# Sparse attention with all operands padded to the full 128x128 array, and one compressed-branch product for both groups

## The chip, the cores and the metric

One NeuronCore of a Trainium2 chip runs the whole layer in one launch. The metric is the device time of the program in microseconds; lower is better. The engines are TensorE (PE; its weight loads are listed as PEld), VectorE (DVE), ScalarE (ACT), GpSimd (POOL) and SyncE (SP), which here only starts transfers.

## The reference

A decoder layer over 256 tokens of width 2048, batch 1: a layer norm, then one projection into three head groups, their outputs joined and projected back, a layer norm, a convolutional feed-forward part (width 5632), a layer norm. The three groups are a gated linear recurrence (1024 channels), sparse attention (8 query heads of width 64 that share 2 key/value groups g), and cross-attention into 256 memory tokens (4 heads of width 128).

The sparse attention has, for each head, three branches: over compressed blocks of keys and values, over selected blocks, and over a window. With 256 tokens there are 4 blocks to select and 16 may be chosen, and the window is 512 wide, so the last two are both causal attention over all keys, each with its own keys and values:

```python
s_c = jnp.einsum('bghqd,bgnd->bghqn', qc, k_cmp) * scale      # 15 compressed blocks
p_c = masked_softmax(s_c, cmp_end[None, :] <= t[:, None])
o_c = jnp.einsum('bghqn,bgnd->bghqd', p_c, v_cmp)
o = gc[..., 0:1] * o_c + gc[..., 1:2] * o_s + gc[..., 2:3] * o_w
```

## The kernel before

All large weights stream through PE in chunks of 128x1024 fp32 (`chunk`, `run`). SyncE loads a chunk into `raw`; ScalarE rounds it to `wH` (L127), VectorE takes the rest `wL = raw - wH` (L135), two chunks ahead of use. The activations are split in the same way, and each product is made of three: high by high (L194), high weight by low activation (L195), low weight by high activation (L197). A chunk of the projection is 8 tiles of 128x128, each with 256 moving columns: 24 products. The L205, L206 and L208 products do the same with the activations as stationary operand.

Attention work is written as Python generators that are put into the list `bg`. After each chunk `pump` takes one step of each live generator, oldest first, and admits one new one, so the steps of several heads stand in one round, behind one chunk. The order of every engine's instructions follows from this by construction; engines wait for one another only by semaphores.

A head of the sparse attention (`nsa_head`, for 128 queries q, group g and head j within the group) has five steps: the score products (L675, and L676, which adds the causal mask by an identity matrix), softmax (L680 to L684), scaling by sum and gate (L686 to L689), transposes (L695) and their copy to `PT`, value products (L704) into the output bank `outs[q]`. Score products use 64 rows of the array, since a head is 64 wide: group 0 lies in partitions 0 to 63, group 1 in 64 to 127. Value products use 64 columns, since they write the 64 partitions of their group. A plain fp32 product is issued as two passes, a transpose as one. The second 128 queries have twice the keys and so four value products instead of two. There are 16 heads in all (8 for each half of the queries). The first of a half opens the output bank by a product with zeros (L701).

The compressed branch (`nsa_cmp`, for q and g) works in the same five steps: mask (L641) and four score products over 15 blocks (L643), softmax, scaling into `pc`, one transpose (L659), ScalarE copies of its four diagonal blocks into `pcd`, one value product for the four heads of the group (L664). The step of group 1 then splits the finished bank `outs[q]` into `oH` and `oL`. The PSUM tiles concerned are `sc` (two banks), `tp` (two) and `o` (one). The order of the generators is: eight heads of the first half as their queries arrive (`done_q`), two compressed, eight heads of the second half, two compressed, four memory heads.

Keys, values, compressed keys and compressed values are put in place by `done_kk`, `done_vg` and `cmp_rest`. The buffer `lruI` holds memory tokens at first, and later an operand of the recurrence. The kernel's last lines write zeros into a few buffers ahead of all work and convert masks on GpSimd.

Of the kernel before, what the change touches and what calls it, by code (L numbers as in the profile page):

```python
# [21 lines left out]
F32 = mybir.dt.float32  # L22
F32R = mybir.dt.float32r
BF = mybir.dt.bfloat16
AF = mybir.ActivationFunctionType
OP = mybir.AluOpType
AX = mybir.AxisListType
# [3 lines left out]
S = 256  # L31
# [24 lines left out]
def hymba_layer(ctx, tc, x, memT, params, rows, wab, w1, wmem, win, wvg, wout, wup, wdn, out):  # L56
    nc = tc.nc
    V, A, G, T = nc.vector, nc.scalar, nc.gpsimd, nc.tensor

    fix = ctx.enter_context(tc.tile_pool(name="fix", bufs=1))  # L60
# [17 lines left out]
    negh = fix.tile([128, 1], F32, name="negh")  # L78
    identb = fix.tile([128, 128], BF, name="identb")
    diagb = fix.tile([128, 2, 128], BF, name="diagb")  # L80
    cmaskb = fix.tile([128, 2, 60], BF, name="cmaskb")
    ident = prm[:, _P["ident"]]

    def P(name, i=0, n=1):
        s = _P[name].start + i
        return prm[:, s:s + n] if s < NP1 else prm2[:, s - NP1:s - NP1 + n]
# [99 lines left out]
    def split_act(dh, dl, src):  # L186
        A.activation(dh, src, AF.Copy)  # L187
        V.tensor_sub(dl, src, dh.bitcast(F32))  # L188
# [209 lines left out]
    def done_q(a, bank):  # L398
        if a == 0:
            qns[0] = mx.tile([128, 4, S], F32, name="qn")  # L400
        A.activation(qns[0][:, a, :], bank, AF.Copy)
        for g in range(2):
            bg.append(nsa_head(0, g, a))
        if a == 3:
            for g in range(2):
                bg.append(nsa_cmp(0, g))
            for g in range(2):
                for j in range(4):
                    bg.append(nsa_head(1, g, j))
            for g in range(2):  # L410
                bg.append(nsa_cmp(1, g))

    blkt = {}

# [12 lines left out]
                        src[g * 64:g * 64 + 64, hb:hb + 15, :, par],  # L427
                        P(pe, hb * 8, 8)[q][:, None, :].to_broadcast([64, 15, 8]), op=OP.add)

    kk = mx.tile([128, 2, S], F32, name="kk")  # L430

    def done_kk(a, bank):
        A.activation(kk[:, a, :], bank, AF.Copy)

    vv = mx.tile([128, 2, 256], F32, name="vv")
    gates = mx.tile([128, 2, 24], F32, name="gates")
    vacc = {}

    def done_vg():
        for m in range(2):  # L440
            A.activation(vv[:, m, :], vacc[m][:, :256], AF.Copy)
        for m in range(2):
            A.activation(gates[:, m, :], vacc[m][:, 256:NVG], AF.Exp, scale=-1.0)
        V.tensor_scalar(gates, gates, 1.0, None, op0=OP.add)
        V.reciprocal(gates, gates)
# [14 lines left out]


    kcmp = mx.tile([128, 32], F32, name="kcmp")
    vcmp = mx.tile([128, 2, 64], F32, name="vcmp")
    hidv = mx.tile([64, 2, 4, 32], F32, name="hidv")
    hidk = mx.tile([64, 32], F32, name="hidk")

    def cmp_mm(a):
# [8 lines left out]
    def cmp_rest(a, ps):  # L476
        if a == 0:
            A.activation(hidk[:, :30], ps[:64, :30], AF.Gelu_apprx_tanh)
        else:
            for g in range(2):  # L480
                A.activation(hidv[:, g, :, 0:15],
                             ps[:64, g * 15:(g + 1) * 15][:, None, :].to_broadcast([64, 4, 15]), AF.Gelu_apprx_tanh)
        yield
        ps2 = pp.tile([128, 512], F32, name="tp", bufs=2)
        if a == 0:
            T.matmul(ps2[:, :30], P("w2k", 0, 128)[:64], hidk[:, :30], start=True, stop=True)
            V.tensor_copy(kcmp[:, :30], ps2[:, :30])
        else:
            for g in range(2):
                T.matmul(ps2[:, g * 64:(g + 1) * 64], hidv[:, g].rearrange("p j n -> p (j n)"),  # L490
                         P("w2v", 0, 64)[:64], start=True, stop=True, skip_group_check=True)
            V.tensor_copy(vcmp, ps2[:, :128].rearrange("p (g d) -> p g d", g=2))
        yield


# [136 lines left out]
    def nsa_gates(q, g):  # L632
        return gates[:, q, g * 12:(g + 1) * 12].rearrange("p (j c) -> p j c", c=3)

    def nsa_cmp(q, g):
        qn = qns[0]
        rows_ = slice(g * 64, g * 64 + 64)
        qs = slice(q * 128, (q + 1) * 128)
        s = pp.tile([128, 512], F32, name="sc", bufs=2)
        sv = s[:, :60].rearrange("p (j n) -> p j n", j=4)  # L640
        T.matmul(s[:, :60], identb, cmaskb[:, q, :], start=True, stop=False, skip_group_check=True)  # L641
        for j in range(4):
            T.matmul(sv[:, j, :], qn[rows_, j, qs], kcmp[rows_, g * 15:(g + 1) * 15], start=False, stop=True,  # L643
                     skip_group_check=True)
        yield
        w = sm.tile([128, 12], F32, name="cw")
        cs = sm.tile([128, 4, 15], F32, name="cs", bufs=2)
        V.reduce_max(w[:, 0:4], sv, axis=AX.X)
        V.tensor_tensor(cs, sv, w[:, 0:4][:, :, None].to_broadcast([128, 4, 15]), op=OP.subtract)
        A.activation(cs, cs, AF.Exp, scale=NSA_SCALE)  # L650
        yield
        V.reduce_sum(w[:, 4:8], cs, axis=AX.X)
        V.reciprocal(w[:, 4:8], w[:, 4:8])
        V.scalar_tensor_tensor(w[:, 8:12], w[:, 4:8], P("cvalid", q), nsa_gates(q, g)[:, :, 0], op0=OP.mult, op1=OP.mult)
        V.tensor_tensor(pc.rearrange("p (j n) -> p j n", j=4)[:, :, :15], cs,
                        w[:, 8:12][:, :, None].to_broadcast([128, 4, 15]), op=OP.mult)
        yield
        tp = pp.tile([128, 4, 128], F32, name="tp", bufs=2)
        T.transpose(tp[:, 0, :], pc, ident)  # L659
        for j in range(4):  # L660
            r = slice(j * 32, j * 32 + 32)
            A.activation(pcd[r, j, :], tp[r, 0, :], AF.Copy)
        yield
        T.matmul(outs[q][rows_], vcmp[:, g, :], pcd, start=False, stop=True, skip_group_check=True)  # L664
        if g == 1:
            split_act(oH[:, 8:12, q * 128:(q + 1) * 128], oL[:, 8:12, q * 128:(q + 1) * 128], outs[q])
        yield

    def nsa_head(q, g, j):
        qn = qns[0]  # L670
        rows_ = slice(g * 64, g * 64 + 64)
        qs = slice(q * 128, (q + 1) * 128)
        nk = (q + 1) * 128
        s = pp.tile([128, 2, S], F32, name="sc", bufs=2)
        T.matmul(s[:, :, :nk], qn[rows_, j, qs], kk[rows_, :, :nk], start=True, stop=False, skip_group_check=True)  # L675
        T.matmul(s[:, :, nk - 128:nk], identb, diagb, start=False, stop=True, skip_group_check=True)  # L676
        yield
        w = sm.tile([128, 10], F32, name="sw", bufs=6)
        e = mx.tile([128, 2, S], F32, name="P", bufs=5)
        V.reduce_max(w[:, 0:2], s[:, :, :nk], axis=AX.X)  # L680
        V.tensor_scalar(w[:, 2:4], w[:, 0:2], -NSA_SCALE, None, op0=OP.mult)
        for b in range(2):
            A.activation(e[:, b, :nk], s[:, b, :nk], AF.Exp, bias=w[:, 2 + b:3 + b], scale=NSA_SCALE,
                         accum_out=w[:, 4 + b:5 + b])  # L684
        yield
        V.reciprocal(w[:, 6:8], w[:, 4:6])  # L686
        V.tensor_mul(w[:, 8:10], w[:, 6:8], nsa_gates(q, g)[:, j, 1:3])
        for b in range(2):
            V.tensor_scalar(e[:, b, :nk], e[:, b, :nk], w[:, 8 + b:9 + b], None, op0=OP.mult)  # L689
        yield  # L690
        tp = pp.tile([128, 4, 128], F32, name="tp", bufs=2)
        n = 2 * (q + 1)
        for b in range(2):
            for k in range(q + 1):
                T.transpose(tp[:, b * (q + 1) + k, :], e[:, b, k * 128:(k + 1) * 128], ident)  # L695
        pT = mx.tile([128, 4, 128], F32, name="PT", bufs=3)
        A.activation(pT[:, :n], tp[:, :n], AF.Copy)
        yield
        if q not in outs:
            outs[q] = pp.tile([128, 4, 128], F32, name="o", bufs=1)  # L700
            T.matmul(outs[q].rearrange("p a b -> p (a b)"), zb[:, :128], zb, start=True, stop=False, skip_group_check=True)  # L701
        for b in range(2):
            for k in range(q + 1):
                T.matmul(outs[q][rows_, j, :], vv[:, k, b * 128 + g * 64:b * 128 + g * 64 + 64],  # L704
                         pT[:, b * (q + 1) + k, :], start=False, stop=(b == 1 and k == q), skip_group_check=True)
        yield


# [218 lines left out]
    load_part(0, 1)  # L927
    mem_load(0, 2, 2)
    state["load"] = 1
    zb = mx.tile([1, 512], BF, name="zb")  # L930
    V.memset(zb, 0.0)
    V.memset(pcd, 0.0)
    V.memset(pc, 0.0)
    V.memset(hidv, 0.0)
# [9 lines left out]
    G.dma_start(wabt, wab)  # L944
    G.tensor_copy(identb, ident)
    G.tensor_copy(diagb, P("diag", 0, 256).rearrange("p (a b) -> p a b", a=2))
    G.tensor_copy(cmaskb, P("cmask", 0, 120).rearrange("p (a b) -> p a b", a=2))
    run(n_mem + 6, 0)
    bg.append(gain_bias(V, True))
    bg.append(lru_consts())  # L950
    width["n"] = 2
# [119 lines left out]
```

## Time and profile before

| | |
|---|---|
| median of 3 runs | 1147.9 us (1147.19 to 1149.84) |
| profiled execution: device time | 1146.88 us |
| its span, first to last instruction | 1145.1 us |
| granted TensorE clock, mean | 0.995 |
| PE, DVE, ACT, POOL busy | 98%, 64%, 49%, 1% of the span |
| sparse attention's products | 106.9 to 222 us |

Times in rows are microseconds from the start of the span. Products on PE are pipelined: the record of one lasts until its result is written, so records overlap, and how fast PE goes is read from the distance between their starts. A merged row (x8) runs from its first start to its last end.

### The profile page before, as it was taken

Reading aid. Unit: us, or ns where it says so; the run is one execution under the profiler, and the core shown is the slowest. Engines: PE = TensorE matmul, PEld = TensorE weight load, DVE = VectorE, ACT = ScalarE, POOL = GpSimd, SP = SyncE. Lnnn points to the kernel's source line nnn. Section 1 sums busy time; section 2 is a strip of 40 time slices with the busy share of each in tenths; the row PEclk is TensorE's granted clock in tenths of the full one; section 3 lists DMA queues with packets and bytes.
Section 4 is the critical chain, followed back from the end, with each engine's and each line's share of the span. In section 5 each row is a group of like instructions: output and inputs, shape, how many; then the busy total and the mean of one; then the engine's idle time right before and its main releaser. Section 6 shows DMA issues by size and latency. Waiting matters only on the chain. (4 is left out here: it accounts for less than half of the span.)

```text
span 1145.1 us, 19315 instructions
## 1 busy us (share of the span) xinstructions
PE 1120.7 (98%) x7848; PEld 1029.3 (90%) x7848; DVE 734.6 (64%) x1073; ACT 565.3 (49%) x829; POOL 15.3 (1%) x26
## 2 busy tenths in 40 slices
PE   8999999999999899999999999999999999999996
PEld 7889878899988799999999999999999888888884
DVE  6778645567856776666666666666666845454546
ACT  5744444567744555555555555555555433343440
POOL 0200000000000000000000000000000000000000
PEclk9999999999999999999999999999999999999998
DMA  9666322344566466556565656555555776666662
GB/s 339 236 230 218 112 92 93 110 148 151 175 196 181 144 244 197 184 185 188 181 200 176 201 183 198 184 185 186 182 199 179 227 244 197 189 191 193 188 197 93
DMA packets 58984, 211.81 MB, mean 185 GB/s; under 512 B 6544, under 2 KB 6672, under 8 KB 58768
## 3 DMA queue, kind: packets, MB, share of 16 engines
q1 hardware_dynamic: 57024, 203.25, 54.9%
q0 software_dynamic: 1872, 7.34, 1.9%
q8 instruction: 61, 1.00, 0.4%
q14 instruction: 27, 0.22, 0.1%
HBM read 208.47 MB, written 2.10 MB: 184 GB/s over the span
## 5 line engine op out<-in xcount | busy, mean ns | idle before, releaser
L135 DVE TENSOR_TENSOR wL<-raw,wH 128x1024 fp32r<-128x1024 f32 (+2 forms) x367 | 441.5, 1215 | 163.0 <-PE sc L208 118.4
L127 ACT ACTIVATE wH<-raw 128x1024 fp32r<-128x1024 f32 (+2 forms) x367 | 375.6, 1046 | 200.2 <-PE sc L206 163.7
L194 PE MATMUL acc<-h,wH 128*128 128x256 f32 x1152 | 281.1, 284 | 1.4 <-ACT h L187 1.4
L195 PE MATMUL acc<-h,wH 128*128 128x256 f32 x1152 | 276.1, 279 | 0.7 <-DVE h L188 0.7
L194 PEld LDWEIGHTS acc<-h,wH 128*128 128x128 f32 x1152 | 216.7, 188 | 2.1 <-ACT h L187 1.6
L195 PEld LDWEIGHTS acc<-h,wH 128*128 128x128 f32 x1152 | 217.3, 189 | 1.4 <-DVE h L188 1.1
L194 PE MATMUL sc<-h,wH 128*128 128x256 f32 x704 | 168.5, 280 | 0.0
L195 PE MATMUL sc<-h,wH 128*128 128x256 f32 x704 | 168.3, 279 | 0.0
L197 PE MATMUL acc<-h,wL 128*128 128x256 f32 x1152 | 158.8, 279 | 0.0
L197 PEld LDWEIGHTS acc<-h,wL 128*128 128x128 f32 x1152 | 145.3, 188 | 0.0
L195 PEld LDWEIGHTS sc<-h,wH 128*128 128x128 f32 x704 | 132.7, 188 | 0.0
L194 PEld LDWEIGHTS sc<-h,wH 128*128 128x128 f32 x704 | 131.8, 187 | 0.0
L197 PE MATMUL sc<-h,wL 128*128 128x256 f32 x704 | 97.4, 279 | 0.0
L877 DVE SCALAR_TENSOR_TENSOR tn<-sc,prm,tn 128x255 f32<-128x255 f32 x88 | 42.4, 482 | 82.6 <-ACT tn L874 81.0
L197 PEld LDWEIGHTS sc<-h,wL 128*128 128x128 f32 x704 | 89.0, 188 | 0.0
L877 DVE SCALAR_TENSOR_TENSOR tn<-acc,prm,tn 128x255 f32<-128x255 f32 x88 | 42.4, 482 | 44.1 <-ACT tn L874 42.5
L205 PE MATMUL sc<-wH,actH 128*128 128x512 f32 x168 | 66.0, 393 | 0.0
L205 PE MATMUL acc<-wH,actH 128*128 128x512 f32 x168 | 66.0, 393 | 0.0
L206 PE MATMUL acc<-wH,actL 128*128 128x512 f32 x168 | 65.7, 391 | 0.0
L206 PE MATMUL sc<-wH,actL 128*128 128x512 f32 x168 | 65.7, 391 | 0.0
L874 ACT ACTIVATE tn<-sc,prm 128x256 f32<-128x256 f32 x44 | 24.8, 564 | 63.4 <-PE sc L197 63.4
L208 PE MATMUL sc<-wL,actH 128*128 128x512 f32 x168 | 51.9, 390 | 0.0
(294 smaller groups left out, 1213.1 us busy)
## 6 DMA issues: line engine op xcount, KB each, us to landing
raw<-in_wup_dram SPq DMA_DIRECT2D x176, 512.0 KB, 4.3
raw<-in_wdn_dram SPq DMA_DIRECT2D x88, 512.0 KB, 4.3
raw<-in_win_dram SPq DMA_DIRECT2D x56, 512.0 KB, 3.3
raw<-in_wout_dram SPq DMA_DIRECT2D x32, 512.0 KB, 4.2
raw<-in_wmem_dram SPq DMA_DIRECT2D x15, 512.0 KB, 6.9
raw<-in_wvg_dram SPq DMA_DIRECT2D x5, 420.0 KB, 4.1
res<-in_x_dram SPq DMA_DIRECT2D x4, 512.0 KB, 7.6
g<-in_rows_dram POOLq DMA_DIRECT2D x4, 512.0 KB, 6.2
```

The source lines that it names most:

```text
L127: A.activation(h[:, s], raws[j][:, s], AF.Copy)
L135: V.tensor_sub(l[:, s], r[:, s], splits[j][0][:, s].bitcast(F32))
L194: T.matmul(acc, w, hH(kt), start=(first and a == 0), stop=False, skip_group_check=True)
L195: T.matmul(acc, w, hL(kt), start=False, stop=False, skip_group_check=True)
L197: T.matmul(acc, l[:, a * 128:(a + 1) * 128], hH(kt), start=False, stop=(last and a == n - 1), skip_group_check=True)
L205: T.matmul(acc, xh(kt, ms), h[:, w], start=(first and a == 0), stop=False)
L206: T.matmul(acc, xl(kt, ms), h[:, w], start=False, stop=False)
L208: T.matmul(acc, xh(kt, ms), l[:, a * N:(a + 1) * N], start=False, stop=(last and a == n - 1))
L874: A.activation(t, src, AF.Identity, scale=P("fcw", cb * 3 + 2), bias=P("fcb", cb))
L877: V.scalar_tensor_tensor(t[:, s:], src[:, :S - s], P("fcw", cb * 3 + k), t[:, s:], op0=OP.mult, op1=OP.add)
```

## The change

Every sparse-attention operand gets the full size of the array. Keys are kept once for each group, with zeros in the other group's 64 partitions, and all 128 partitions of the queries are used. Values get 128 columns for each group, zeros in the other group's 64, so that a value product writes all 128 partitions of the output and adds zero to the other group's. The buffer for them is `lruI`, cleared in between. Compressed keys are laid out as a 128 by 30 block-diagonal, compressed values as 128 by 128, so that one generator does both groups. The first value product of a half starts the accumulation, and the products with zeros are gone.

```diff
-            for g in range(2):
-                bg.append(nsa_cmp(0, g))
+            bg.append(nsa_cmp(0))
...
-    kk = mx.tile([128, 2, S], F32, name="kk")
+    kk = mx.tile([128, 2, 2, S], F32, name="kk")
+    V.memset(kk, 0.0)
     def done_kk(a, bank):
-        A.activation(kk[:, a, :], bank, AF.Copy)
+        for g in range(2):
+            r = slice(g * 64, g * 64 + 64)
+            A.activation(kk[r, g, a, :], bank[r], AF.Copy)
...
+    def vv_zero():
+        vvs[0] = mx.tile([128, 2, 2, 2, 128], F32, name="lruI")
+        V.memset(vvs[0], 0.0)
...
     def done_vg():
         for m in range(2):
-            A.activation(vv[:, m, :], vacc[m][:, :256], AF.Copy)
+            src = vacc[m][:, :256].rearrange("p (b g d) -> p b g d", b=2, g=2)
+            for g in range(2):
+                A.activation(vvs[0][:, g, m, :, g * 64:g * 64 + 64], src[:, :, g, :], AF.Copy)
...
-            V.tensor_copy(kcmp[:, :30], ps2[:, :30])
+            for g in range(2):
+                r = slice(g * 64, g * 64 + 64)
+                V.tensor_copy(kcmp[r, g * 15:(g + 1) * 15], ps2[r, g * 15:(g + 1) * 15])
...
-    def nsa_cmp(q, g):
+    def nsa_cmp(q):
-        T.matmul(s[:, :60], identb, cmaskb[:, q, :], start=True, stop=False, skip_group_check=True)
+        T.matmul(s[:, :120], identb, cmaskb[:, q].rearrange("p j g n -> p (j g n)"), start=True, stop=False,
+                 skip_group_check=True)
         for j in range(4):
-            T.matmul(sv[:, j, :], qn[rows_, j, qs], kcmp[rows_, g * 15:(g + 1) * 15], start=False, stop=True,
+            T.matmul(s[:, j * 30:(j + 1) * 30], qn[:, j, qs], kcmp[:, :30], start=False, stop=True,
                      skip_group_check=True)
...
-        T.matmul(outs[q][rows_], vcmp[:, g, :], pcd, start=False, stop=True, skip_group_check=True)
-        if g == 1:
-            split_act(oH[:, 8:12, q * 128:(q + 1) * 128], oL[:, 8:12, q * 128:(q + 1) * 128], outs[q])
+        T.matmul(outs[q].rearrange("p a b -> p (a b)"), vcmp, pcd.rearrange("p a b -> p (a b)"), start=False, stop=True,
+                 skip_group_check=True)
+        split_act(oH[:, 8:12, q * 128:(q + 1) * 128], oL[:, 8:12, q * 128:(q + 1) * 128], outs[q])
...
-        T.matmul(s[:, :, :nk], qn[rows_, j, qs], kk[rows_, :, :nk], start=True, stop=False, skip_group_check=True)
+        T.matmul(s[:, :, :nk], qn[:, j, qs], kk[:, g, :, :nk], start=True, stop=False, skip_group_check=True)
...
-            T.matmul(outs[q].rearrange("p a b -> p (a b)"), zb[:, :128], zb, start=True, stop=False, skip_group_check=True)
...
-                T.matmul(outs[q][rows_, j, :], vv[:, k, b * 128 + g * 64:b * 128 + g * 64 + 64],
-                         pT[:, b * (q + 1) + k, :], start=False, stop=(b == 1 and k == q), skip_group_check=True)
+                T.matmul(outs[q][:, j, :], vvs[0][:, g, k, b, :], pT[:, b * (q + 1) + k, :],
+                         start=(first and b == 0 and k == 0), stop=(b == 1 and k == q), skip_group_check=True)
...
-    zb = mx.tile([1, 512], BF, name="zb")
-    V.memset(zb, 0.0)
+    V.memset(kcmp, 0.0)
...
-    G.tensor_copy(cmaskb, P("cmask", 0, 120).rearrange("p (a b) -> p a b", a=2))
+    for g in range(2):
+        G.tensor_copy(cmaskb[:, :, :, g, :], P("cmask", 0, 120).rearrange("p (q j n) -> p q j n", q=2, j=4))
     run(n_mem + 6, 0)
+    vv_zero()
```

The softmax and scaling of the compressed branch run on 128x120 instead of twice on 128x60, with the same instructions.

## Rows read from the trace of the kernel before

**Rows 1.** The page: PE's busy time, and the granted clock in 40 slices.

```profile
PE 1120.7 (98%) x7848; PEld 1029.3 (90%) x7848; DVE 734.6 (64%) x1073; ACT 565.3 (49%) x829; POOL 15.3 (1%) x26
PEclk9999999999999999999999999999999999999998
```

**Rows 2.** Busy time of each engine in one stretch; granted clock, DMA share, GB/s.

```profile
106.00:240.00 134.00, 133.05 (x946) 111.03 (x945) 81.24 (x195) 66.84 (x167) 0.00 (x0) 1.00 0.34 111
```

**Rows 3.** PE's waits in the whole span: us in total, times, longest.

```profile
PE sc L675 <- ACT qn L401: 0.9, 2, 0.5
```

**Rows 4.** Timeline of PE, one round: start, us, engine, line, operation, names, form, count.

```profile
126.09 1.09 PE L197 MATMUL acc<-h,wL 128*128 128x256 f32 x8
127.11 0.65 PE L704 MATMUL o<-PT,vv 128*64 128x128 f32 x4
127.69 0.44 PE L695 MATMUL tp<-prm,P 128*128 128x128 f32 x2
128.06 0.70 PE L675 MATMUL sc<-kk,qn 64*128 64x256 f32 x2
128.69 0.28 PE L676 MATMUL sc<-diagb,identb 128*128 128x256 bf16 x1
...
128.93 0.28 PE L195 MATMUL acc<-h,wH 128*128 128x256 f32 x1
```

**Rows 5.** Timeline of PE: transposes straight behind a chunk.

```profile
117.31 1.10 PE L197 MATMUL acc<-h,wL 128*128 128x256 f32 x8
118.24 0.38 PE L695 MATMUL tp<-prm,P 128*128 128x128 f32 x2
```

**Rows 6.** Timeline of PE: full-size steps of the memory heads.

```profile
226.39 1.03 PE L560 MATMUL o<-PT,vmem 128*128 128x256 f32 x4
227.25 0.60 PE L554 MATMUL tp<-prm,P 128*128 128x128 f32 x4
```

**Rows 7.** Timeline of PE: the score step of a compressed branch.

```profile
141.75 0.19 PE L641 MATMUL sc<-cmaskb,identb 128*128 128x60 bf16 x1
141.87 1.06 PE L643 MATMUL sc<-kcmp,qn 64*128 64x15 f32 x8
142.86 0.39 PE L194 MATMUL acc<-h,wH 128*128 128x256 f32 x1
143.08 0.28 PE L195 MATMUL acc<-h,wH 128*128 128x256 f32 x1
```

**Rows 8.** Timeline of PE: the round in which the second output bank is opened.

```profile
170.76 1.10 PE L197 MATMUL acc<-h,wL 128*128 128x256 f32 x8
171.79 0.38 PE L701 MATMUL o<-zb 1*128 1x512 bf16 x1
172.11 1.09 PE L704 MATMUL o<-PT,vv 128*64 128x128 f32 x8
```

**Rows 9.** Timeline of PE: the value step of a compressed branch.

```profile
160.79 1.07 PE L664 MATMUL o<-pcd,vcmp 128*64 128x512 f32 x2
161.80 0.33 PE L659 MATMUL tp<-prm,pc 128*128 128x128 f32 x1
```

**Rows 10.** Timeline of DVE: a clear at the start, and the stretch before 83 us.

```profile
1.21 0.48 DVE L932 MEMSET pcd<- 128x512 f32 x1
...
4.75 0.69 DVE L188 TENSOR_TENSOR oL<-lruR,oH 128x512 fp32r<-128x512 f32 x1 [2.65 <-ACT oH L187]
...
82.50 0.19 DVE L487 COPY kcmp<-tp 128x30 f32<-128x30 f32 x1 [3.92 <-PE tp L486]
```

**Rows 11.** Timeline of DVE and PE: a split weight piece, and its first product.

```profile
98.44 1.22 DVE L135 TENSOR_TENSOR wL<-raw,wH 128x1024 fp32r<-128x1024 f32 x1
...
102.49 0.75 PE L197 MATMUL acc<-h,wL 128*128 128x256 f32 x5
```

**Rows 12.** Timeline of ACT and PE: exponentials, and the score that reuses their bank.

```profile
187.90 0.46 ACT L683 ACTIVATE P<-sc,sw 128x256 f32<-128x256 f32 x1
...
190.73 1.12 PE L675 MATMUL sc<-kk,qn 64*128 64x512 f32 x2
```

More of the change, by code (lines that the diff above doesn't have):

```diff
@@ L80, in hymba_layer @@
     diagb = fix.tile([128, 2, 128], BF, name="diagb")
-    cmaskb = fix.tile([128, 2, 60], BF, name="cmaskb")
+    cmaskb = fix.tile([128, 2, 4, 2, 15], BF, name="cmaskb")
     ident = prm[:, _P["ident"]]
@@ L409, in done_q @@
                     bg.append(nsa_head(1, g, j))
-            for g in range(2):
-                bg.append(nsa_cmp(1, g))
+            bg.append(nsa_cmp(1))
     blkt = {}
@@ L428, in done_cmp @@
                         P(pe, hb * 8, 8)[q][:, None, :].to_broadcast([64, 15, 8]), op=OP.add)
-    kk = mx.tile([128, 2, S], F32, name="kk")
+    kk = mx.tile([128, 2, 2, S], F32, name="kk")
+    V.memset(kk, 0.0)
     def done_kk(a, bank):
-        A.activation(kk[:, a, :], bank, AF.Copy)
-    vv = mx.tile([128, 2, 256], F32, name="vv")
+        for g in range(2):
+            r = slice(g * 64, g * 64 + 64)
+            A.activation(kk[r, g, a, :], bank[r], AF.Copy)
+    vvs = {}
+    def vv_zero():
+        vvs[0] = mx.tile([128, 2, 2, 2, 128], F32, name="lruI")
+        V.memset(vvs[0], 0.0)
     gates = mx.tile([128, 2, 24], F32, name="gates")
@@ L462, in hymba_layer @@
     kcmp = mx.tile([128, 32], F32, name="kcmp")
-    vcmp = mx.tile([128, 2, 64], F32, name="vcmp")
-    hidv = mx.tile([64, 2, 4, 32], F32, name="hidv")
+    vcmp = mx.tile([128, 128], F32, name="vcmp")
+    hidv = mx.tile([64, 2, 4, 2, 16], F32, name="hidv")
     hidk = mx.tile([64, 32], F32, name="hidk")
@@ L480, in cmp_rest @@
             for g in range(2):
-                A.activation(hidv[:, g, :, 0:15],
+                A.activation(hidv[:, g, :, g, 0:15],
                              ps[:64, g * 15:(g + 1) * 15][:, None, :].to_broadcast([64, 4, 15]), AF.Gelu_apprx_tanh)
@@ L486, in cmp_rest @@
             T.matmul(ps2[:, :30], P("w2k", 0, 128)[:64], hidk[:, :30], start=True, stop=True)
-            V.tensor_copy(kcmp[:, :30], ps2[:, :30])
+            for g in range(2):
+                r = slice(g * 64, g * 64 + 64)
+                V.tensor_copy(kcmp[r, g * 15:(g + 1) * 15], ps2[r, g * 15:(g + 1) * 15])
         else:
             for g in range(2):
-                T.matmul(ps2[:, g * 64:(g + 1) * 64], hidv[:, g].rearrange("p j n -> p (j n)"),
+                T.matmul(ps2[:, g * 64:(g + 1) * 64], hidv[:, g].rearrange("p j a n -> p (j a n)"),
                          P("w2v", 0, 64)[:64], start=True, stop=True, skip_group_check=True)
-            V.tensor_copy(vcmp, ps2[:, :128].rearrange("p (g d) -> p g d", g=2))
+            V.tensor_copy(vcmp, ps2[:, :128])
         yield
@@ L633, in nsa_gates @@
         return gates[:, q, g * 12:(g + 1) * 12].rearrange("p (j c) -> p j c", c=3)
-    def nsa_cmp(q, g):
+    def nsa_cmp(q):
         qn = qns[0]
-        rows_ = slice(g * 64, g * 64 + 64)
         qs = slice(q * 128, (q + 1) * 128)
         s = pp.tile([128, 512], F32, name="sc", bufs=2)
-        sv = s[:, :60].rearrange("p (j n) -> p j n", j=4)
-        T.matmul(s[:, :60], identb, cmaskb[:, q, :], start=True, stop=False, skip_group_check=True)
+        sv = s[:, :120].rearrange("p (a n) -> p a n", n=15)
+        T.matmul(s[:, :120], identb, cmaskb[:, q].rearrange("p j g n -> p (j g n)"), start=True, stop=False,
+                 skip_group_check=True)
@@ L642, in nsa_cmp @@
         for j in range(4):
-            T.matmul(sv[:, j, :], qn[rows_, j, qs], kcmp[rows_, g * 15:(g + 1) * 15], start=False, stop=True,
+            T.matmul(s[:, j * 30:(j + 1) * 30], qn[:, j, qs], kcmp[:, :30], start=False, stop=True,
                      skip_group_check=True)
         yield
[L646 to L649, printed above, removed]
+        w = sm.tile([128, 24], F32, name="cw", bufs=2)
@@ L650, in nsa_cmp @@
+        cs = sm.tile([128, 8, 15], F32, name="cs", bufs=2)
+        V.reduce_max(w[:, 0:8], sv, axis=AX.X)
+        V.tensor_tensor(cs, sv, w[:, 0:8][:, :, None].to_broadcast([128, 8, 15]), op=OP.subtract)
         A.activation(cs, cs, AF.Exp, scale=NSA_SCALE)
         yield
[L652 to L656, printed above, removed]
+        V.reduce_sum(w[:, 8:16], cs, axis=AX.X)
@@ new lines, in nsa_cmp @@
+        V.reciprocal(w[:, 8:16], w[:, 8:16])
+        V.scalar_tensor_tensor(w[:, 16:24].rearrange("p (j g) -> p j g", j=4),
+                               w[:, 8:16].rearrange("p (j g) -> p j g", j=4), P("cvalid", q),
+                               gates[:, q, :].rearrange("p (g j c) -> p j g c", g=2, c=3)[:, :, :, 0],
+                               op0=OP.mult, op1=OP.mult)
+        V.tensor_tensor(pc.rearrange("p (a n) -> p a n", n=16)[:, :, :15], cs,
+                        w[:, 16:24][:, :, None].to_broadcast([128, 8, 15]), op=OP.mult)
@@ L670, in nsa_head @@
         qn = qns[0]
-        rows_ = slice(g * 64, g * 64 + 64)
         qs = slice(q * 128, (q + 1) * 128)
@@ L698, in nsa_head @@
         yield
-        if q not in outs:
+        first = q not in outs
+        if first:
             outs[q] = pp.tile([128, 4, 128], F32, name="o", bufs=1)
-            T.matmul(outs[q].rearrange("p a b -> p (a b)"), zb[:, :128], zb, start=True, stop=False, skip_group_check=True)
         for b in range(2):
             for k in range(q + 1):
-                T.matmul(outs[q][rows_, j, :], vv[:, k, b * 128 + g * 64:b * 128 + g * 64 + 64],
-                         pT[:, b * (q + 1) + k, :], start=False, stop=(b == 1 and k == q), skip_group_check=True)
+                T.matmul(outs[q][:, j, :], vvs[0][:, g, k, b, :], pT[:, b * (q + 1) + k, :],
+                         start=(first and b == 0 and k == 0), stop=(b == 1 and k == q), skip_group_check=True)
         yield
```

## The prediction, made before the change was run

> **What bounds the kernel now.** I read the busy shares first: TensorE (PE) is busy 1120.7 of 1145.1 us, at the full granted clock in nearly every slice [rows 1]. Then the busy times of the stretch in which the sparse attention runs, 106 to 240 us: PE 133.05 of 134 us, VectorE 81.24, ScalarE 66.84, and the DMA engines at 0.34 [rows 2]. Then PE's waits: in that stretch only the first score products wait, for the copy of the queries out of PSUM, 0.9 us in two times [rows 3]. So PE sets the time there, and what shortens its own sequence shortens the kernel, as long as nothing else becomes late. A "busy" PE is not an efficient one, though: its products' records overlap, so I read the distances between their starts in the timeline. This is where the reader should look longest.
>
> One round (a weight chunk, and behind it one step of each live head) shows it. The chunk's last run L197 has 8 products in 1.09 us, the last 0.28 long: (1.09 - 0.28)/7 = 0.116 us from start to start, and the last starts at 126.09 + 1.09 - 0.28 = 126.90. The value products, 128 rows by 64 columns, start 0.21 later, not 0.116. Their four passes take to 127.69, the two transposes (full array) to 128.06, the score (64 rows) to 128.69, and the chunk's second product stands at 128.93 [rows 4]. Where a full-size transpose follows a full-size product directly, the distance is 118.24 - (117.31 + 1.10 - 0.28) = 0.11 us [rows 5]. So it is not the step, nor its semaphore, that costs the extra time, but the change of the used part of the array: PE finishes what is in it (0.09), and then the first weight load stands open instead of running under the product before. The score shows both: 0.63 from its start to the mask is two passes of 0.214 (priced below), 0.09 and a load of 0.11. The values' 0.58 is four passes of 0.109, 0.09 and 0.05; the transposes' 0.37 is two of 0.109, 0.09 and 0.06.
>
> **The change part by part.** Prices in full size, from rows: a transpose (0.60 - 0.27)/3 = 0.109; a pass of 256 fp32 columns (1.03 - 0.38)/3 = 0.217 [rows 6], which I take as 0.214, the next start not being slowed by a change; a short pass bound by its weight load, (1.06 - 0.26)/7 = 0.114, with the first one's exposed load in it, so 0.113 [rows 7]. The padded value pass (128 columns loaded, 128 streamed) does not occur before: below, 0.109 as the transposes; above, 0.117 as a chunk product; I take 0.113, since its load has the same 128 fp32 columns as the short pass.
>
> *Heads.* The round of rows 4, from 126.90 to 128.93, is 2.03; less two chunk distances of 0.116 its steps cost 1.80. Padded: 4 x 0.113 + 2 x 0.109 + 2 x 0.214 + 0.11 (mask) = 1.21. Saved: 0.59. There are 16 heads, each with one such set: 9.44. Off it: the score steps that wait for the queries anyway [rows 3] keep their entry under that wait, 2 x 0.20; the second eight heads have 8 value passes instead of 4, 32 more at 0.004 = 0.13; two later scores that come just as the queries are ready, 0.14 together. Left: 8.8 us.
>
> *The two zero products* L701 that opened the output bank go. From the last chunk start (170.76 + 1.10 - 0.28 = 171.58) to the value product at 172.11 is 0.53, where a round without them has 0.21: 0.32 each [rows 8], together 0.64.
>
> *Compressed branch.* Four steps become two. Score part: from the mask at 141.75 to the second chunk product at 143.08, 1.33 - 0.116 = 1.21 [rows 7]; in full size 9 x 0.113 = 1.02 for both groups. 4 x 1.21 - 2 x 1.02 = 2.8. Value part: 160.79 to 161.80 is 1.01, with 0.09 on entry and 0.05 behind it, 1.15 [rows 9]; in full size 512 columns in two passes, 2 x 0.43. 4 x 1.15 - 2 x 0.86 = 2.9. Two transposes less: 0.2. Sum 5.9 us.
>
> *Off PE.* The blocks of zeros must be written. VectorE clears 128x1024 for the keys at the start, and less for kcmp: 128x512 took 0.48, so about 0.97; it then waits 2.65 us for the first ScalarE result, and covers it [rows 10]. It clears 128x1024 for the values around 77 us, ahead of 3.92 us of its own idle time [rows 10]. If both covers failed, they would cost 2 us. kcmp is copied in two pieces (+0.2), in the part in which VectorE is fullest; there a split weight piece, done at 98.44 + 1.22 = 99.66, is first read at 102.49, 2.8 us later [rows 11]. ScalarE copies keys and values in more pieces (about 1 us in all, the gates later by 0.4), and saves eight of sixteen small copies of the compressed branch. GpSimd casts the mask twice, some 85 us before it is used. None of this is on PE's path: cost nothing, up to 2 us.
>
> *What is late next.* Rounds become 0.6 us shorter, so each step comes sooner behind the softmax of the round before. The closest pair: the exponentials that free a score bank end at 187.90 + 0.46 = 188.36, and the score that reuses it comes at 190.73, 2.37 us later [rows 12]. Two rounds lie between, which take 1.2 of it at most. The hand-over of the one output bank from the first 128 queries to the second keeps its distance, since a whole round still lies between the compressed product and the next head's first value product. So no wait takes the place of the drains. The weights' DMA has room at 0.34 [rows 2].
>
> *The sum:* 8.8 + 0.64 + 5.9 = 15.3 us. The profiled execution took 1146.88 with a span of 1145.1, so it would go to 1131.6. The median of the runs, 1147.9, is 1.0 above it: 1132.6.
>
> A rule speaks against this sum. The chunk's products, all of full height, show the next weight load running under the present product: 8 in 1.09 us, 0.116 apart, where load and stream one after the other would take about twice that [rows 4]. The Trainium skill, "TensorE: Matmul & The Clock Gate", Part 3 (Packing small matmuls), says that a weight load overlaps a running product only when it goes to another group of rows. By that rule a full-height operand would give up the overlap; by the row it does not. The case is a rival below.
>
> **Rivals.**
> 1. *Only the drains go, the loads stay open,* because the padded steps come from another buffer or dtype than the chunks. For: where a drain goes, the load behind it has not been seen to hide in these very forms. Against: transposes after a chunk start at 0.11 [rows 5]. A head then loses 0.05 + 0.05 + 0.107 + 0.02 = 0.23 of its 0.59: 16 x 0.23 = 3.7, saving 11.6, time 1136.3.
> 2. *Full-height loads don't overlap at all in plain fp32.* The rule of the Trainium skill above would make this the general case. Each of the 96 value passes would be 0.107 + 0.109 instead of 0.113, +9.9; each of the 32 score passes +0.107, +3.4. Saving 2.0, time 1145.9. Against: four fp32 passes of full size stand 0.217 apart [rows 6], which is 256 columns with nothing added.
> 3. *The gaps don't belong to the array's shape* and stay. Then only fewer products count: zero products 0.64, compressed score 2 x 1.21, value 2 x 1.15, transposes 0.2, less the wider value passes 0.4: 5.2, time 1142.7. Against: rows 5 beside rows 4.
> 4. *Softmax becomes the pacer.* VectorE is at 81 of 134 us, so its work alone doesn't, but its order may: if its chain kept its present dates, the 2.37 us of [rows 12] would be eaten after four rounds, and about 2.4 + 5.9 would be left of the gain: 1139.6.
> 5. *Slower:* with fuller operands TensorE's granted clock falls to its lower level (1.2 of 2.4 GHz) in the stretch 106 to 240 us. Each microsecond spent there holds half of the work, so from 31 us at that level (15.3 us lost) on, the kernel is slower; the whole stretch would cost over 100 us. Against: the clock is 1.00 there [rows 2], PE is never idle long, and the change takes idle time away.
>
> **How the numbers follow.** Forecast 0.81, the first rival 0.07, the second 0.02, the third 0.03, the fourth 0.05, the fifth 0.02. The forecast's own bounds: value passes at 0.109 or 0.117 move it by 0.4 either way, uncovered clears cost up to 2, and medians of this kernel scatter by about a microsecond: 1130.5 to 1135.5. The range goes on to the first rival: 1130.5 to 1137. A difference of 0.2%, 2.3 us, is what a measurement here can tell from none. The second rival (1145.9) is within it; the fifth is slower; all the others are faster: 0.95 faster, 0.03 the same, 0.02 slower.
>
> **What would show it.** In the profile after: value, transpose and score follow the chunk and one another at 0.11 to 0.12 us, with no weight-load gap between them; a round with one of each of the first eight heads has steps of about 1.2 us where 1.8 stood; value passes 0.113 apart; two compressed score runs of 8 passes, and two value runs of 2; no L701; what follows the sparse attention starts 15 us earlier, and all behind it is shifted as a block. It is wrong if PE shows new idle time in front of these steps, with VectorE or ScalarE as the releaser, or if the 15 us are given back after 240 us, where a weight that comes too late would show as PE waiting for ScalarE's or VectorE's split.

## The result, and the profile after

The changed kernel takes 1141.98 us (median of 4 executions, 1141.22 to 1143.44); the kernel before took 1148.87 beside it. The ratio is 0.9935, 95% interval 0.9912 to 0.9958: 7 us faster, where 15.3 were forecast, and outside my range of 1130.5 to 1137. The profiled execution took 1143.44.

The page of the changed kernel, its span and its busy times [rows 1]:

```profile
span 1141.7 us, 19259 instructions
PE 1115.1 (98%) x7822; PEld 1033.4 (91%) x7822; DVE 734.9 (64%) x1064; ACT 562.9 (49%) x823; POOL 15.5 (1%) x27
```

The attention stretch did what was forecast. Its timeline on PE, one round with a value, a transpose and a score step, and the compressed score step; the counterparts of [rows 4, 7]:

```profile
132.45 1.10 PE L197 MATMUL acc<-h,wL 128*128 128x256 f32 x8
133.39 0.61 PE L718 MATMUL o<-PT,lruI 128*128 128x128 f32 x4
133.83 0.38 PE L709 MATMUL tp<-prm,P 128*128 128x128 f32 x2
134.05 0.67 PE L689 MATMUL sc<-kk,qn 128*128 128x256 f32 x2
134.56 0.27 PE L690 MATMUL sc<-diagb,identb 128*128 128x256 bf16 x1
134.79 0.28 PE L195 MATMUL acc<-h,wH 128*128 128x256 f32 x1
...
185.59 0.60 PE L709 MATMUL tp<-prm,P 128*128 128x128 f32 x4
186.03 0.22 PE L652 MATMUL sc<-cmaskb,identb 128*128 128x120 bf16 x1
186.08 1.03 PE L655 MATMUL sc<-kcmp,qn 128*128 128x30 f32 x8
186.95 0.36 PE L194 MATMUL acc<-h,wH 128*128 128x256 f32 x1
187.15 0.28 PE L195 MATMUL acc<-h,wH 128*128 128x256 f32 x1
```

The value step starts 133.39 - (132.45 + 1.10 - 0.28) = 0.12 after the chunk's last product, where it was 0.21; four value passes take 0.44, two transposes 0.22, against 0.58 and 0.37. From the last chunk product (133.27) to the second of the next chunk (134.79) the round needs 1.52, less two chunk distances 1.29; before, it was 1.80. In this round the score step takes 0.51 to its mask instead of 0.43, 0.08 late, as was expected in two rounds whose queries have only just arrived; the round before it and the round after it need 1.21, the forecast's number. The compressed score step needs 187.15 - 186.03 = 1.12, less one chunk distance 1.00 for both groups, where 1.02 was forecast.

The weight loads of the round before it, on PE's load side:

```profile
129.24 0.53 PEld L718 LDWEIGHTS o<-PT,lruI 128*128 128x128 f32 x4
129.69 0.25 PEld L709 LDWEIGHTS tp<-prm,P 128*128 128x128 f32 x2
129.91 0.30 PEld L689 LDWEIGHTS sc<-kk,qn 128*128 128x128 f32 x2
130.24 0.10 PEld L690 LDWEIGHTS <-identb 128*128 128x128 bf16 x1
```

The first of them starts 0.01 after the chunk's last product does (129.23), so it runs under that product, and no row has an idle time in brackets. In the round of [rows 4], the kernel before had three such times on its load side:

```profile
127.69 0.20 PEld L695 LDWEIGHTS tp<-prm,P 128*128 128x128 f32 x2 [0.17 <-issue]
128.06 0.29 PEld L675 LDWEIGHTS sc<-kk,qn 64*128 64x128 f32 x2 [0.17 <-issue]
128.69 0.10 PEld L676 LDWEIGHTS <-identb 128*128 128x128 bf16 x1 [0.33 <-issue]
```

This settles the rule of the Trainium skill that the prediction set against the sum ("TensorE: Matmul & The Clock Gate", Part 3): full-height loads do overlap here.

So where did 8 us go? I compared the starts of the same chunk product, counted from the first, in both traces. Product 600 (103 us) is 3.8 us late in the changed kernel; product 1300 (243 us), behind the attention, is 11.1 us early: 14.9 us gained in between. Up to product 2300 (421 us) it is 12.2 early. Then the lead shrinks evenly, by 0.11 us in each 100 products of the up stage and by 0.44 in each 100 of the down stage, to 3.6 at the end. No wait stands in these stages; every product comes a little later behind the one before it. A view that shows it is the count of PE's products in equal windows. Of the kernel before, in the first 80 us, the out, the up and the down stage (columns: window, PE busy and count, loads, VectorE, ScalarE, GpSimd, granted clock, DMA share, GB/s):

```profile
60.00:80.00 20.00, 18.27 (x168) 17.70 (x167) 14.64 (x29) 8.57 (x14) 0.00 (x0) 1.00 0.67 237
325.00:370.00 45.00, 45.00 (x194) 36.27 (x193) 25.12 (x25) 17.95 (x17) 0.00 (x0) 1.00 0.64 188
450.00:850.00 400.00, 400.00 (x3431) 400.00 (x3430) 264.02 (x357) 206.03 (x287) 0.00 (x0) 1.00 0.59 190
950.00:1100.00 150.00, 150.00 (x657) 123.05 (x657) 75.27 (x67) 57.90 (x55) 0.00 (x0) 1.00 0.64 192
```

Of the changed kernel, the same windows:

```profile
60.00:80.00 20.00, 17.78 (x148) 17.18 (x148) 14.41 (x30) 8.91 (x13) 0.00 (x0) 0.91 0.63 234
325.00:370.00 45.00, 45.00 (x198) 36.94 (x197) 28.00 (x27) 19.69 (x19) 0.00 (x0) 1.00 0.68 210
450.00:850.00 400.00, 400.00 (x3399) 400.00 (x3398) 262.74 (x354) 204.07 (x283) 0.00 (x0) 1.00 0.59 187
950.00:1100.00 150.00, 150.00 (x645) 120.21 (x644) 70.43 (x62) 56.47 (x54) 0.00 (x0) 1.00 0.62 189
```

PE is "busy" all the time in both, at the full clock. In the up stage it does 3399 products in 400 us instead of 3431: 0.1177 us each instead of 0.1166. In the down stage it is 645 instead of 657: 0.233 instead of 0.228. In the out stage it is faster: 198 instead of 194. (A window also counts a product that only reaches into it. From start to start, averaged over hundreds of products, the distances are 0.1178 and 0.1167 in the up stage, 0.2333 and 0.2289 in the down stage; these are used from here on.)

The first 80 us have a loss of another kind. Behind a wait of 1.58 us for the last normalised activations the granted clock falls to the lower of its two levels (1.2 of 2.4 GHz; 0.50 from 70 to 72 us, 0.91 over the window), and PE's waits for the first weights add up to 6.6 us instead of 5.4. It does not go with the change: the profiled executions of e3_wpad and e4_apad below, which compute as the kernel before, have the same fall of the clock (0.91), while e1_held, which computes as the changed kernel, has none and is only 0.3 us late at product 600. The other three executions of the changed kernel had spans of 1139.4 to 1140.3, against 1141.7 here.

### The profile page after: what moved, and what is told of

It reads as the page before. It is cut to its first block, busy times and chain, and to the rows that moved or that the text cites. A ratio compares the mean times of both kernels' runs of the same rounds, so it can differ in the third digit from the quotient of the medians.

```text
span 1141.7 us, 19259 instructions
## 1 busy us (share of the span) xinstructions
PE 1115.1 (98%) x7822; PEld 1033.4 (91%) x7822; DVE 734.9 (64%) x1064; ACT 562.9 (49%) x823; POOL 15.5 (1%) x27
## 5 line engine op out<-in xcount | busy, mean ns | idle before, releaser
L208 PE MATMUL acc<-wL,actH 128*128 128x512 f32 x168 | 52.7, 394 | 0.0
```

The lines of the kernel that those rows point to most:

```text
L208: T.matmul(acc, xh(kt, ms), l[:, a * N:(a + 1) * N], start=False, stop=(last and a == n - 1))
```

## The experiments

What differs in the later stages, in which the change edits nothing? The compiled program's buffer addresses. The wider mask makes its buffer larger, and the softmax buffers of the compressed branch too; the weights `raw`, `wH`, `wL` lie 224 bytes further in each partition, the activations `oH`, `actH` 608 bytes. `h`, allocated first, stays. Theory A: the distance between products depends on these addresses. Theory B: it belongs to the execution, or to the earlier arrival.

**Addresses held (e1_held).** The whole change at the old addresses:

```diff
-    cmaskb = fix.tile([128, 2, 4, 2, 15], BF, name="cmaskb")
+    fix.tile([128, 120], BF, name="cmaskb")
...
+    zb = mx.tile([128, 512], BF, name="zb")
+    state["mask"] = zb[:, :240].rearrange("p (q j g n) -> p q j g n", q=2, j=4, g=2)
...
-        cs = sm.tile([128, 8, 15], F32, name="cs", bufs=2)
+        cs = sm.tile([128, 8, 15], F32, name="cs", bufs=1)
+        sm.tile([128, 24], F32, name="cpad", bufs=1)
```

> The whole change, but every buffer of weights and activations at the address that it has in the kernel before (the wider mask lies in the place of the zero row, and a pad keeps the sizes). In the changed kernel the weights lie 224 bytes further and the activations 608. Theory A (addresses): the distance between the products of the up stage falls back from 0.1178 to 0.1167 us and that of the down stage from 0.233 to 0.229, so the 15 us of the attention stretch stay: 1133 to 1135 us, ratio to before 0.987. Theory B (the products' rate belongs to the run, or to the earlier arrival at the stages): distances as in the changed kernel, 1140 to 1142, ratio 0.994.

Measured: 1133.38 us (1132.61 to 1139.01), ratio 0.9872 (0.984 to 0.9904). Its up and down stage are those of the kernel before:

```profile
450.00:850.00 400.00, 400.00 (x3431) 400.00 (x3431) 264.66 (x357) 205.43 (x286) 0.00 (x0) 1.00 0.58 188
950.00:1100.00 150.00, 150.00 (x657) 123.15 (x656) 72.33 (x63) 58.41 (x56) 0.00 (x0) 1.00 0.63 192
```

Theory A holds, and the change itself is worth what was forecast for it: 1132.6 against 1133.38, and 15.4 us less than the kernel before beside it (1148.81). One of its four executions took 1139.01.

**The kernel before at other addresses (e2_moved, e3_wpad, e4_apad).** Pads of 224 bytes in `fix`, of 384 in `sm`, or both:

```diff
+    fix.tile([128, 56], F32, name="fpad")
...
+        sm.tile([128, 96], F32, name="cpad", bufs=1)
```

In e2_moved the zero row goes too, and the zero product reads a zero of the identity.

> The kernel before, with pads that put all weights and activations where the changed kernel has them, and the zero product fed from a zero in the identity matrix. Theory A: up stage at 0.1178, down stage at 0.233, out stage faster at 0.229: 7 to 9 us slower than before, about 1157, ratio 1.007. Theory B: as before, within 2 us of 1148.9.

Measured: median 1155.76, ratio 1.004 (1.0007 to 1.0072); 3399, 644 and 198 products in the windows of up, down and out, as in the changed kernel. Nine of ten executions took 1154.5 to 1157.2, one 1139.92, which no theory here explains.

> The kernel before with one pad of 224 bytes behind the mask: weights and activations move by 224 together, only the residual-stream operand h stays. Theory A, if what counts is where the two operands of a product lie towards each other: the up stage (weights against h) goes to 0.1178, 4.5 us more; the down stage (weights against activations that moved as much) stays at 0.229: ratio 1.004. If each operand's own place within 64 bytes counts: down goes to 0.233 too, 9 us more, ratio 1.008. Theory B: no change.

Measured: 1154.51 (1154.37 to 1155.13), ratio 1.0041 (1.0022 to 1.0061). Up has 3399 products, down 657, out 195: only up is slower. Moving weights and activations together leaves the distance between their products as it was, which speaks for the place of the two operands towards each other.

> The kernel before with one pad of 384 bytes behind the weights' buffers: only the activations of the out and the down stage move. Theory A with the operands' relative place: up stays at 0.1167, down goes to 0.233 (4.7 us more), out to 0.229 (1.7 us less): ratio 1.003. If each operand's own place within 64 bytes counts: no change, since 384 is a multiple of 64. Theory B: no change.

Measured: 1151.45, ratio 1.0023 (1.0011 to 1.0036). Down 645, out 198, as expected from the relative place. But up had 3399 in the profiled execution, whose 1157.08 us were the longest of ten; the median is what 3431 in up would give. One execution can thus differ: here h and the weights lie where the kernel before has them, and its up stage still runs at the slower distance. I have stage counts of one execution of each kernel only.

**Only h moved (e8_w0, f1_h32_w0, f2_h32_w224),** and the best placement (e5_best). These have the whole change, with pads ahead of the weights, and 128 bytes ahead of `oH` and of the activations' pool, so that weights minus activations is 64 modulo 256 (the remainder after division by 256) in out and down. The residual rows and the masks behind h move with it; in the windows counted here no product reads them:

```diff
+    fix.tile([128, 8], F32, name="hpad")      # f1, f2: ahead of h
     hq = [fix.tile([128, 4, S], F32R, name="h%d" % i) for i in range(8)]
...
+    fix.tile([128, 8], F32, name="fpad")      # e5, f1: 32 bytes; e8_w0: 64; f2: none
...
+    mx.tile([128, 32], F32, name="mpad")
     oH = mx.tile([128, KT, S], F32R, name="oH")
...
         cs = sm.tile([128, 8, 15], F32, name="cs", bufs=2)
+        sm.tile([128, 32], F32, name="cpad", bufs=1)
```

> The whole change with three pads: 32 bytes ahead of the weights (they start at 224 modulo 256 again, as in the kernel before), and 128 bytes each ahead of the activations of the down and of the out stage, so that weights minus activations is 64 modulo 256 in both; in the kernel before it was 64 in down and 192 in out. Theory A (the relative place of the two operands sets the distance between products): up 0.1167, down and out 0.229: the time of e1_held less 1.7 in the out stage, 1131 to 1132.5, ratio 0.9855. Theory B' (only the very addresses of the kernel before are good): up 0.1178, 1136 to 1141.

Measured: 1131.2 us (1130.35 to 1132.58), ratio 0.9837 (0.9806 to 0.9867): below both kernels. 3431, 657 and 198 products: all three stages at their faster distance.

> e5_best with the weights (and all behind them) 32 bytes further: weights at 0 modulo 256, the relation in down and out unchanged. Theory A1 (an odd multiple of 32 between weights and h is what the up stage needs): up at 0.1178, 4.5 us more than e5_best. Theory A2 (only some other relation is slow): up at 0.1167, as e5_best. Down and out at 0.229 by both.

Measured: 1148.05, ratio 0.9989 (0.9974 to 1.0004): 32 bytes take the whole gain away. Its up stage, the down stage untouched:

```profile
450.00:850.00 400.00, 400.00 (x3336) 400.00 (x3335) 257.26 (x348) 200.83 (x279) 0.00 (x0) 1.00 0.58 183
950.00:1100.00 150.00, 150.00 (x657) 123.08 (x656) 74.72 (x67) 57.31 (x55) 0.00 (x0) 1.00 0.63 192
```

From start to start that is 0.1200 us. Neither A1 nor A2 had said that the slow value would be a third one, with three times the loss (0.0033 us a product instead of 0.0011). Of the 16.9 us between the medians of e8_w0 and e5_best, the two traces show 13.4 in the up stage; the chunks of the projection read h as well, and products 600 to 1300 take 1.8 us longer.

> e8_w0 (weights at 0 modulo 256, up stage at 0.1200) with only the residual-stream operand h moved by 32 bytes. Theory A-relative (what counts is h minus weights, which is 32 now as in the kernel before): up back at 0.1167, 1131 to 1132. Theory A-weights (the weights' own place counts): up stays at 0.1200, 1148. If each placement draws its own value without a rule: anything between.

Measured: 1130.58 (1129.59 to 1130.98), ratio 0.9833 (0.9791 to 0.9874). The weights lie where e8_w0 has them; h moved by 32 bytes:

```profile
450.00:850.00 400.00, 400.00 (x3431) 400.00 (x3430) 265.51 (x359) 205.98 (x287) 0.00 (x0) 1.00 0.59 189
```

> e5_best (weights at 224, up stage at 0.1167) with only h moved by 32 bytes. Theory A-relative (h minus weights is 64 now, as in the changed kernel): up at 0.1178, 1135.7. Theory A-weights: up stays at 0.1167, 1131.

Measured: 1137.05 (1136.11 to 1138.27), ratio 0.9891 (0.9849 to 0.9934). The weights lie where e5_best has them:

```profile
450.00:850.00 400.00, 400.00 (x3398) 400.00 (x3398) 261.37 (x353) 203.57 (x283) 0.00 (x0) 1.00 0.59 187
```

So, in these executions, it is the relative place: with h minus weights at 32 modulo 256 an up product takes 0.1167, at 64 0.1178, at 0 0.1200, whichever of the two was moved. (In the kernel before and in e5_best the difference itself is 256 bytes apart, at the same 0.1167.) In the up stage h is read by PE alone. The other engines' traffic in the weights' buffers does not explain it either: of 4000 up products of the changed kernel, 3509 have VectorE or ScalarE busy between their start and the next one's, 491 have neither, and both groups stand 0.1178 apart. That points to two reads of PE, that of the moving operand and that of the next weights; where they meet is not shown.

**The other places (e8_w32, e8_w64, e8_w96, e8_w128),** pads of 96, 128, 160 and 192 bytes ahead of the weights:

> e5_best with the weights at 64 modulo 256 against h at 0; down and out keep their relation of 64. Measured so far in the up stage: 224: 0.1167, 192: 0.1178, 0: 0.1200 us between products. Theory A1 (an odd multiple of 32 is needed): 64 is slow, 0.1178 to 0.1200, 1136 to 1148. Theory A3 (the nearer the two starts modulo 256, the slower, with 0 the worst): 64 like 192, 0.1178, 1136. Theory A4 (only the same place modulo 256 is slow, the rest is drift): 0.1167, 1131.

> The same with the weights at 96 modulo 256. Theory A1: fast, 0.1167, 1131. Theory A3: fast or faster, 1131 or less. Theory A4: 1131.

> The same with the weights at 128 modulo 256. Theory A1: slow, 0.1178 to 0.1200, 1136 to 1148. Theory A3: the farthest place, so the fastest, at or under 0.1167, 1131 or less. Theory A4: 1131.

> The same with the weights at 32 modulo 256. Theory A1: fast, 0.1167, 1131. Theory A3: between 0 and 64, 0.119, 1141. Theory A4: 1131.

Measured: w32 3383 products in the up window, 1139.74 us; w64 3399, 1136.85; w96 3373, 1138.66 (1134.78 to 1147.45 over eight executions); w128 3373, 1141.02. A1 fails (weights at 32 and 96, odd multiples, are slow), A3 fails (the farthest place is not fast), A4 fails. Of the seven places measured (weights at 160 were not tried) only one, h minus weights at 32, gives the up stage 0.1167. But the relative place is not the whole rule. In w64 the out stage had 195 products although its relation was 64. And in the same trace the projection's chunks, with h and the weights' buffers where they also are in the up stage, begin at a distance that no up stage had, and later run at that of its up stage:

```profile
106.80 0.28 PE L196 MATMUL acc<-h,wH 128*128 128x256 f32 x1
...
108.51 1.07 PE L198 MATMUL acc<-h,wL 128*128 128x256 f32 x8
...
254.32 0.28 PE L195 MATMUL acc<-h,wH 128*128 128x256 f32 x1
...
256.21 1.11 PE L198 MATMUL acc<-h,wL 128*128 128x256 f32 x8
```

The first pair is 15 products apart, 0.114 us each; the second 16, 0.118 each.

**The price of the shapes (e6_score64, e7_value64).** One step of a head put back to its small shape in e1_held:

```diff
-        T.matmul(s[:, :, :nk], qn[:, j, qs], kk[:, g, :, :nk], ...
+        T.matmul(s[:, :, :nk], qn[g * 64:g * 64 + 64, j, qs], kk[g * 64:g * 64 + 64, g, :, :nk], ...
```

```diff
-                T.matmul(outs[q][:, j, :], vvs[0][:, g, k, b, :], pT[:, b * (q + 1) + k, :],
+                T.matmul(outs[q][g * 64:g * 64 + 64, j, :], vvs[0][:, g, k, b, g * 64:g * 64 + 64], pT[:, b * (q + 1) + k, :],
```

> e1_held with the score products back on the 64 rows of their group (the same keys and queries, sliced). If entering and leaving the 64-row form costs the drain and the open load that I read from the kernel before: 13 entries behind transposes at 0.20, one uncovered entry behind a chunk at 0.19, 16 exits to the mask at 0.11: 4.6 us more than e1_held, 1138. If the gaps did not belong to the array's shape: as e1_held.

Measured: 1139.11 (1137.95 to 1143.87), 5.7 more than e1_held. The score step of a round, on PE:

```profile
129.44 0.38 PE L710 MATMUL tp<-prm,P 128*128 128x128 f32 x2
129.75 0.70 PE L690 MATMUL sc<-kk,qn 64*128 64x256 f32 x2
130.38 0.28 PE L691 MATMUL sc<-diagb,identb 128*128 128x256 bf16 x1
```

> e1_held with the value products back on the 64 columns of their group (each group's first one opens its half of the bank). Entering and leaving: 16 x (0.14 + 0.15) = 4.6, less 96 passes that are 0.004 shorter: 4.3 us more than e1_held, 1137.7. If the gaps did not belong to the shape: 0.4 less than e1_held.

Measured: 1138.63 (1137.95 to 1139.03), 5.3 more. The value step:

```profile
130.96 1.09 PE L197 MATMUL acc<-h,wL 128*128 128x256 f32 x8
131.99 0.65 PE L720 MATMUL o<-PT,lruI 128*64 128x128 f32 x4
132.57 0.44 PE L710 MATMUL tp<-prm,P 128*128 128x128 f32 x2
132.84 0.60 PE L690 MATMUL sc<-kk,qn 128*128 128x256 f32 x2
```

The score takes 0.63 to its mask and the transposes before it 0.31; the values take 0.58, entered at 0.22, and the transposes behind them 0.27: the numbers of [rows 4] come back with the shape, each for itself. Summed over all rounds, the steps of e6 cost 4.2 us more on PE than those of e1_held, those of e7 4.3, against 4.6 and 4.3 expected. The medians differ by more; against the kernel before beside each it is 5.2 and 4.7, and the profiled executions of e6 and e7 have the early fall of the clock (0.91 from 60 to 80 us) that e1_held's has not. The third rival (the gaps do not belong to the shape) is out.

## Why the prediction was wrong

The sum of the change's own terms was right. Heads, zero products and compressed branch were to give 15.3 us; between products 600 and 1300 the traces show 14.9, 15.2 with the addresses held, and that kernel comes to 1133.38 where 1132.6 was forecast. The drains, the open loads, the value passes at 0.11 and the two rounds in which the queries are only just there came as worked out; no wait took their place, and none of the five rivals happened. That the measured 1141.98 lies beside the third rival's 1142.7 is a coincidence: the gaps went, as the rounds show.

The step that failed stands under "Off PE": "None of this is on PE's path: cost nothing, up to 2 us". I priced the wider buffers by the instructions that fill them, and they cost nothing as instructions. That they also push every later buffer to another address was not a term at all, and the last part's "all behind it is shifted as a block" rested on that. It measured: 0.0011 us for each of the 4224 up products, so that the lead shrinks by 4.3 us from the first up product to the first down product; 0.0044 for each of the 1056 down products, 4.2 us of lead; less about 1.3 gained in out. That is 7 us, half of the gain. I looked for a give-back as a wait for weights; it came with PE never idle. The range, 1130.5 to 1137, holds for the change at held addresses; nothing in it stood for a rate of the other 800 us, although e8_w0 shows that 32 bytes can cost 17.

What stays open: why one place of the seven is fast in the up stage and the others are not; why a stage can hold another distance in another execution (e4_apad's longest, e2_moved's 1139.92); and the out stage and the projection of e8_w64.

## What to carry to other kernels

Between small-shape steps on TensorE, count the changes of shape, not only the products: here each cost 0.11 to 0.20 us, and padding the score and value steps with zeros cost less (e6_score64, e7_value64). When an edit changes the size of any buffer, compare the addresses of all others before and after, and the distance between products in stages that the edit does not touch. A stage in which PE is 100% busy at full clock can still be some per cent off: count its products in a fixed window.

## What the runs showed of the hardware

The mean distance between 128x128 fp32r products with 256 moving columns was 0.1167, 0.1178, 0.1183, 0.1187 or 0.1200 us in the up stage, the same over thousands of products of an execution. It changed with the address of the moving operand minus that of the weights (f1_h32_w0 and f2_h32_w224 moved the former against e8_w0 and e5_best), though the same addresses could also hold another distance (e4_apad, e8_w64). With 512 columns it was 0.2289 or 0.2333. The Trainium skill says that loading the next weights takes no SBUF read bandwidth from the running product ("TensorE: Matmul & The Clock Gate", Part 2), and that TensorE's ports never wait on anyone ("SBUF — State Buffer", SBUF: two separate sides). By these sentences the distance should not depend on how the two operands lie towards each other. In the runs here it does, at a price of 1 to 3%, and the measurement decides; that the two reads meet is the likely reading, not a shown one.
